# A hybrid encoder layer in split precision: both parts of the moving operand in one matmul

## The chip, the cores and the metric

The kernel runs on one core of a Trainium2 chip. The metric is the device time of one execution in microseconds (us), lower is better.

## The reference

One layer, 512 tokens, width 2048, float32. Three blocks with plain residual adds, each behind an RMSNorm, and a last RMSNorm:

```python
x = x + concat([gated_delta_net(h), short_conv(h)]) @ w_mix_out      # h = rmsnorm(x) @ w_mix_in
# cross-attention into 256 memory tokens, 4 heads of 512
q = h @ w_q;  k = mem_n @ w_k;  v = mem_n @ w_v
x = x + softmax(q @ k.T * 512 ** -0.5) @ v @ w_o
# ConvFFN, d_ff = 5632
u = causal_dwconv(h @ w_up, conv_w)                                  # width 3
x = x + (silu(u[..., :d_ff]) * u[..., d_ff:]) @ w_down
```

## The kernel before, in words

**Split precision.** A float32 operand is split in two: the high part is its rounding to the matmul's 4-byte format `fp32r` (a copy on ScalarE, ACT), the low part the rest (a subtraction on VectorE, DVE). A product is three matmuls into one PSUM bank: high x high, high x low, low x high. `wpiece` (line 133) loads 128 x 1024 weights through SP's DMA queue into one of 5 buffers `wst` and splits them into `whi` and `wlo`, 3 buffers each; `split` (147) does the same for a 128 x 512 tile of activations. `mm3` (153) issues the three matmuls, weights stationary and activations moving; `proj` (158) loops it over the depth.

**Stages.** Memory's K (`mem_proj`, 310; tile `psk`); the product of K and w_xq, "score weights", stored to `wk_d` (loop at 371, tile `pswk`); V (`mem_proj` again); V times w_xo to `mo_d`; the mixer's input projection with the delta net woven between; output projection; scores and softmax; the attention's output projection; the up-projection; the down-projection. In K, V, score weights and the up-projection the moving operand is 256 columns wide, in the other projections 512.

K and V: a bank holds two output blocks of 256 memory tokens each. They are multiplied by memory's norm `rmem` (DVE) and split. K's first three pairs wait for that norm in PSUM. Score weights: one bank of 512 columns per piece of w_xq, scaled by ACT on the way out.

**Up-projection.** A Strassen-like scheme with seven products per unit, on halves of the tokens (`LO`, `HI`, 256 columns each) and halves of the depth. The seven moving operands `xop[1..7]` are made by `up_prepare` (807) during the attention's output projection. The loop over 44 units (line 1050) alternates gate and up columns, a pair of units per tile of the hidden layer. `pair_loads` (844) fetches four weight blocks on SP's queue and forms two sums of weights by accumulating DMAs on GpSimd's (POOL's) queue (lines 853 and 859). A unit's products, each eight triples by `product` (910), run into banks in this order:

```python
px: 1 -> copied;  py: 2;  px += 6 -> copied;  pz: 5 -> copied
px += 7 -> added to pz's copy;  pz += 3;  px += 4
```

Partial sums leave by ACT copies (lines 1064, 1083, 1086: `tq`, `tz`) and DVE adds (1071, 1089, 1093: halves of `ug` and `uu`). `gate_half` (1019) multiplies by the FFN norm `r2`, convolves (`unit_conv`: one ACT and two DVE instructions) and applies Silu; `up_half` (1027) does norm and convolution for the up columns, multiplies by the gate, and on every second unit forms the sums that the down-projection needs; both store to `hf_d` on ACT's queue. Seven weight splits per unit (`wsplit`, 834: lines 837 and 838) run on ACT and DVE meanwhile.

**Order.** Each engine and each DMA queue works through its own list in order. A planner lays these lists out at build time: among the instructions whose inputs it reckons to be ready, by its own costs, it takes the one that stands first in the program. Inside `tc.manual_schedule(engines=...)` the named engines keep the program's order; that holds for PE in K, and for ACT and DVE in the last unit of the up-projection, where the first pieces of the down-projection (`make`, `fac_split`) are placed by hand between its steps.

PSUM has 8 banks: 3 in pool `pm`, 5 in `pg`. Tiles of 128 x 512 come from one pool of 64 (`T`), 56 of which hold `xop` in the up-projection.

Of the kernel before, what the change touches and what calls it, by code (L numbers as in the profile page):

```python
# [69 lines left out]
def trunk(ctx: ExitStack, tc: tile.TileContext, g):  # L70
# [82 lines left out]
    def mm3(ps, wh, wl, xh, xl, first, last):  # L153
        nc.tensor.matmul(ps, wh, xh, start=first, stop=False)  # L154
        nc.tensor.matmul(ps, wh, xl, start=False, stop=False)  # L155
        nc.tensor.matmul(ps, wl, xh, start=False, stop=last)  # L156

    def proj(src, xs, ps, kt=KT, per=8, ready=None):

        for i in range(kt // per):  # L160
            hi, lo = ready[i] if ready else wpiece(src(i))
            for k in range(per):
                kk = i * per + k
                xh, xl = xs[kk]
                mm3(ps, hi[:, k * P : (k + 1) * P], lo[:, k * P : (k + 1) * P], xh, xl, kk == 0, kk == kt - 1)

# [88 lines left out]
    def mem_parts(i):  # L255
        mh, ml = T("mwh", F32R), T("mwl", F32R)
        for k in range(2):
            sl = slice(k * NMEM, (k + 1) * NMEM)
            c = col(C_MEMN + 2 * i + k)
            nc.scalar.activation(mh[:, sl], m2s[i][:, sl], AF.Identity, scale=c)  # L260
            nc.vector.scalar_tensor_tensor(ml[:, sl], m2s[i][:, sl], c, f(mh)[:, sl], op0=ALU.mult, op1=ALU.subtract)
            mws.append((mh[:, sl], ml[:, sl]))

# [46 lines left out]
    def mem_proj(w, begin=False, beside=None):  # L310

        out, held = [], []
        for n2 in range(KT // 2):
            if begin and n2 == 0:
                ps = [PG("psk")[:, :NMEM] for _ in range(2)]
                for i in range(2):
                    for k in range(8):
                        for q in range(2):
                            hi, lo = early[q, 2 * i + k // 4]
                            c = slice(k % 4 * P, (k % 4 + 1) * P)  # L320
                            mm3(ps[q], hi[:, c], lo[:, c], *mws[8 * i + k], i == 0 and k == 0, i == 1 and k == 7)
# [12 lines left out]
            if begin and n2 < 2:  # L334
                continue
            if begin and n2 == 2:
                mem_norm()
            for ps in held:
                t = T("kt")
                for q in range(2):  # L340
                    nc.vector.tensor_tensor(t[:, q * NMEM : (q + 1) * NMEM], ps[q], rmem[:, q], op=ALU.mult)
                th, tl = T("kth", F32R), T("ktl", F32R)
                nc.scalar.copy(th, t)
                nc.vector.tensor_tensor(tl, t, f(th), op=ALU.subtract)
                for q in range(2):
                    out.append((th[:, q * NMEM : (q + 1) * NMEM], tl[:, q * NMEM : (q + 1) * NMEM]))
            held = []
            if beside:
                beside(n2)
        return out  # L350
# [3 lines left out]

    nc.vector.tensor_copy(mk[:, 0, 0:1], f(kts[0][0])[:, 0:1])
# [3 lines left out]
    nc.vector.tensor_copy(idb[:, 0, 0:1], f(kts[0][0])[:, 0:1])  # L359
    nc.sync.dma_start(idb, g["idb"])  # L360
# [8 lines left out]
    for i in range(3):  # L369
        load_x()  # L370
    for i in range(KT):
        load_x()
        add_squares(xacc, xts[i], i == 0)
        wkt = [T("wka"), T("wkb")]
        for q in range(2):
            hi, lo = wpiece(g["w_xq"][i, q])
            ps = PG("pswk")
            for hh in range(2):
                for k in range(4):
                    kk = (2 * q + hh) * 4 + k  # L380
                    kl = hh * 4 + k
                    mm3(ps[:, hh * NMEM : (hh + 1) * NMEM], hi[:, kl * P : (kl + 1) * P], lo[:, kl * P : (kl + 1) * P], kts[kk][0], kts[kk][1], k == 0, k == 3)
            nc.scalar.activation(wkt[q], ps, AF.Identity, scale=col(C_XN + i))
            nc.scalar.dma_start(wk_d[i][:, q * S : (q + 1) * S], wkt[q])
    r0 = rstd_rows([xacc])
# [14 lines left out]
    with tc.manual_schedule(engines={mybir.EngineType.PE}):  # L400
        for hd in range(XH):
            for ng in range(4):
# [4 lines left out]
                for q in range(2):  # L407
                    hi, lo = wpiece(g["w_xo"][hd, ng, q])
                    for mt in range(2):
                        for k in range(2):  # L410
                            kk = q * 2 + k
                            vh, vl = vts[hd * 4 + kk]
                            msl = slice(mt * P, (mt + 1) * P)
# [390 lines left out]

    b11 = []

    def up_prepare(k, xa, xb):
        tt = nc.vector.tensor_tensor
        tc_, td = TB("tc"), TB("td")
        tt(tc_[:, LO], xa[:, HI], xa[:, LO], op=ALU.subtract)  # L810
        tt(tc_[:, HI], xb[:, HI], tc_[:, LO], op=ALU.subtract)
        tt(td[:, LO], xa[:, HI], xb[:, HI], op=ALU.subtract)
        tt(td[:, HI], xb[:, LO], tc_[:, HI], op=ALU.subtract)
        if k % 2 == 0:
            b11[:] = [T("b11h", F32R), T("b11l", F32R)]
        sl = HI if k % 2 else LO
        bh, bl = b11
        nc.scalar.copy(bh[:, sl], xa[:, LO])
        tt(bl[:, sl], xa[:, LO], f(bh)[:, sl], op=ALU.subtract)
        xop[1].append((bh[:, sl], bl[:, sl]))  # L820
        for t, left, right in ((xb, 2, 3), (tc_, 5, 6), (td, 7, 4)):
            th, tl = split(t, "xo")
            xop[left].append((th[:, LO], tl[:, LO]))
            xop[right].append((th[:, HI], tl[:, HI]))

# [84 lines left out]
    def product(ps, w, r, first):  # L910

        hi, lo = w
        for k in range(HK):
            c = slice(k * P, (k + 1) * P)
            xh, xl = xop[r][k]
            nc.tensor.matmul(ps, hi[:, c], xh, start=first and k == 0, stop=False, skip_group_check=True)  # L916
            nc.tensor.matmul(ps, hi[:, c], xl, start=False, stop=False, skip_group_check=True)  # L917
            nc.tensor.matmul(ps, lo[:, c], xh, start=False, stop=k == HK - 1, skip_group_check=True)  # L918

# [91 lines left out]
    def unit_conv(u, t):  # L1011
# [5 lines left out]
        return cv  # L1017

    def gate_half(i, ug):
        tt(ug, ug, r2[0], op=ALU.mult)  # L1020
        cv = unit_conv(ug, i)
# [4 lines left out]

    def up_half(pos, px, uu, gate):
        i, k = up_order[pos], pos // 2
        tt(uu[:, LO], px, r2[0][:, LO], op=ALU.mult)
        tt(uu[:, HI], uu[:, HI], r2[0][:, HI], op=ALU.mult)  # L1030
        cv = unit_conv(uu, NF + i)
# [15 lines left out]
        nc.scalar.dma_start(hf_d[k, 5:7].rearrange("f p s -> p f s"), b.rearrange("p (f s) -> p f s", f=2))  # L1047

    for i in range(NF):
        if i == 1:  # L1050
# [5 lines left out]
        else:  # L1056
            a11, a12, a22, s1, s3, w1, w2 = first
        px = PG("px")[:, :S2]
# [4 lines left out]
        tq, tz = T("tq"), T("tz")  # L1063
        nc.scalar.copy(tq[:, LO], px)
        if i:
            w2 = wsplit(a12)
        py = PM("py")[:, :S2]
        product(py, w2, 2, True)
        turn_rest()
        ug, uu = T("ug"), T("uu")  # L1070
        tt(ug[:, LO], py, tq[:, LO], op=ALU.add)
        if i == 1:
# [9 lines left out]
        product(px, wsplit(s2), 6, False)  # L1082
        nc.scalar.copy(tq[:, HI], px)  # L1083
        pz = PG("pz")[:, :S2]
        product(pz, wsplit(s1), 5, True)
        nc.scalar.copy(tz[:, LO], pz)
        if i < NF - 1:
            product(px, wsplit(s3), 7, False)
            tt(uu[:, HI], px, tz[:, LO], op=ALU.add)
# [3 lines left out]
            tt(ug[:, HI], pz, tq[:, HI], op=ALU.add)  # L1093
            product(px, wsplit(a22), 4, False)
            if not r2:
                r2.append(rstd_rows([acc2]))
            up_half(i, px, uu, gate_half(up_order[i], ug))
            continue

        with tc.manual_schedule(engines={mybir.EngineType.Activation, mybir.EngineType.DVE}):  # L1100
# [4 lines left out]
            fac_split(0, 0)  # L1105
            tt(uu[:, HI], px, tz[:, LO], op=ALU.add)
            product(px, w4, 4, False)
            make(0)
            tt(ug[:, HI], pz, tq[:, HI], op=ALU.add)
            make(1)  # L1110
            gate = gate_half(up_order[i], ug)
            fac_split(0, 1)
            up_half(i, px, uu, gate)

# [188 lines left out]
```

## Time and profile before

| | us |
|---|---|
| median of 3 runs (2791.53 to 2795.15) | 2793.29 |
| the profiled execution | 2792.25 |
| its span, first to last instruction | 2790.4 |
| busy in the span: TensorE (PE) | 2755.7 |
| VectorE (DVE) | 1981.4 |
| ScalarE (ACT) | 1382.8 |
| GpSimd (POOL) | 266.9 |

In the rows of the timeline stand start and duration of an instruction, its engine, line, operation, and output <- inputs with their shapes; in square brackets the idle time of its engine before it, and what ended that. In rows of groups, the count, then busy time and mean ns of one, then idle time before them. In rows of waits: who waited, for whom, us in total, times, longest. Matmuls are pipelined, so that their durations overlap, and the time that one takes of PE is read from start to start. `PEld` is PE's loading of weights, which runs beside the matmuls.

### The profile page before, as it was taken

To read this page: it belongs to the slowest core of one execution; us is meant where nothing else is said; L and a number is where in the kernel's file an instruction comes from. 1 tells how busy PE (TensorE), PEld (TensorE's weight loads), DVE (VectorE), ACT (ScalarE), POOL (GpSimd) and SP (SyncE) were. 2 spreads that over 40 slices of the span, in tenths; PEclk is the share of its full clock that TensorE was granted. 3 is DMA by queue.
4 is the path that set the end of the run, shared out by engine and by line. 5 is a ranking of instruction groups with operands and counts; after the bars stand their busy time and mean duration, and the time that the engine had idled before them with its cause. 6 is when DMAs were issued, how large, how long until landed. Compare 5 with 4: busy or idle time off the path is not lost.

```text
span 2790.4 us, 43956 instructions
## 1 busy us (share of the span) xinstructions
PE 2755.7 (99%) x17277; PEld 2470.8 (89%) x17277; DVE 1981.4 (71%) x2979; ACT 1382.8 (50%) x1944; POOL 266.9 (10%) x258
## 2 busy tenths in 40 slices
PE   9999999999999999999999999999999999999997
PEld 9999878888788888888789999999999998888885
DVE  6546547878774334445678888888888888877877
ACT  6564644345443323234565555555555555454545
POOL 2120001012110000110120000000000000000211
PEclk9999999999999999999999999999999999999999
DMA  7785853333322234445556666676766675764976
GB/s 260 239 281 190 265 179 103 112 94 94 106 91 87 98 98 151 141 145 178 167 167 178 182 178 182 175 194 160 193 171 192 164 190 189 255 191 144 288 229 176
DMA packets 213952, 479.72 MB, mean 172 GB/s; under 512 B 26720, under 2 KB 94192, under 8 KB 213744
## 3 DMA queue, kind: packets, MB, share of 16 engines
q1 hardware_dynamic: 154688, 372.81, 40.6%
q0 software_dynamic: 20272, 62.94, 12.6%
q10 hardware_dynamic: 38784, 41.17, 4.2%
q8 instruction: 135, 2.21, 0.3%
q14 instruction: 73, 0.60, 0.1%
HBM read 424.13 MB, written 52.71 MB: 171 GB/s over the span
## 4 chain that ended last, share of the span: by engine, by line
PE 66%; DVE 2%; DMA 1%; issue 1%; ACT 1%; DVEq 0%; SPq 0%; ACTq 0%
PE px L916 6%; PE px L917 6%; PE px L918 6%; PE psd L1136 4%; PE psd L1134 4%; PE psd L1135 4%; PE pssc L154 3%; PE pssc L156 3%; PE pssc L155 3%; PE psx L155 3%; PE psx L154 3%; PE psx L156 3%; PE pz L918 3%; PE pz L917 3%; PE pz L916 3%; PE py L918 1%
## 5 line engine op out<-in xcount | busy, mean ns | idle before, releaser
L144 DVE TENSOR_TENSOR wlo<-wst,whi 128x1024 fp32r<-128x1024 f32 x316 | 389.2, 1233 | 329.5 <-ACT whi L143 328.6
L143 ACT CAST whi<-wst 128x1024 fp32r<-128x1024 f32 x316 | 331.7, 1051 | 554.6 <-PE pssc L155 140.0
L837 ACT CAST whi<-wst 128x1024 fp32r<-128x1024 f32 x177 | 185.6, 1049 | 271.4 <-PE px L917 143.5
L916 PE MATMUL px<-xoh,whi 128*128 128x256 f32 x1056 | 299.1, 283 | 1.2 <-ACT tq L1083 0.9
L918 PE MATMUL px<-xoh,wlo 128*128 128x256 f32 x1056 | 298.9, 283 | 0.0
L917 PE MATMUL px<-xol,whi 128*128 128x256 f32 x1056 | 298.8, 283 | 0.0
L838 DVE TENSOR_TENSOR wlo<-wst,whi 128x1024 fp32r<-128x1024 f32 x177 | 216.4, 1223 | 70.3 <-ACT whi L837 68.9
L1136 PE MATMUL psd<-wlo,hdh 128*128 128x512 f32 x616 | 241.0, 391 | 7.8 <-DVE wlo L958 7.8
L1135 PE MATMUL psd<-whi,hdl 128*128 128x512 f32 x616 | 239.9, 389 | 0.5 <-DVE hdl L150 0.5
L1134 PE MATMUL psd<-whi,hdh 128*128 128x512 f32 x616 | 239.9, 389 | 0.1
L916 PEld LDWEIGHTS px<-xoh,whi 128*128 128x128 f32 x1056 | 202.7, 192 | 1.8 <-ACT tq L1083 1.1
L917 PEld LDWEIGHTS px<-xol,whi 128*128 128x128 f32 x1056 | 202.7, 192 | 0.0
L918 PEld LDWEIGHTS px<-xoh,wlo 128*128 128x128 f32 x1056 | 202.7, 192 | 0.0
L918 PE MATMUL pz<-xoh,wlo 128*128 128x256 f32 x704 | 199.4, 283 | 0.9 <-DVE wlo L838 0.9
L916 PE MATMUL pz<-xoh,whi 128*128 128x256 f32 x704 | 199.4, 283 | 0.3 <-ACT whi L837 0.3
L917 PE MATMUL pz<-xol,whi 128*128 128x256 f32 x704 | 199.2, 283 | 0.0
L837 ACT CAST whi<-s 128x1024 fp32r<-128x1024 f32 x131 | 137.2, 1048 | 87.3 <-PE px L917 66.8
L955 ACT CAST whi<-wst 128x1024 fp32r<-128x1024 f32 x99 | 104.3, 1054 | 121.7 <-issue 62.5
L838 DVE TENSOR_TENSOR wlo<-s,whi 128x1024 fp32r<-128x1024 f32 x131 | 160.1, 1222 | 0.5 <-ACT whi L837 0.5
L154 PE MATMUL psq<-hh,whi 128*128 128x512 f32 x384 | 155.9, 406 | 0.0
L154 PE MATMUL pssc<-hh,whi 128*128 128x512 f32 x384 | 153.2, 399 | 0.0
L156 PE MATMUL psq<-hh,wlo 128*128 128x512 f32 x384 | 150.2, 391 | 0.0
(364 smaller groups left out, 7640.1 us busy)
## 6 DMA issues: line engine op xcount, KB each, us to landing
wst<-in_w_up SPq DMA_DIRECT2D x132, 512.0 KB, 4.8
wst<-in_w_dn SPq DMA_DIRECT2D x121, 512.0 KB, 4.4
wst<-in_w_mix SPq DMA_DIRECT2D x112, 512.0 KB, 3.4
s<-in_w_up POOLq DMA_DIRECT2D x87, 512.0 KB, 5.8
s<-in_w_up SPq DMA_DIRECT2D x43, 512.0 KB, 4.9
hid<-hf_d SPq DMA_DIRECT2D x77, 256.0 KB, 5.0
wst<-in_w_xq SPq DMA_DIRECT2D x32, 512.0 KB, 5.0
wst<-in_w_xv SPq DMA_DIRECT2D x32, 512.0 KB, 3.5
```

The lines of the kernel that those rows point to most:

```text
L143: nc.scalar.copy(hi, st)
L144: nc.vector.tensor_tensor(lo, st, f(hi), op=ALU.subtract)
L154: nc.tensor.matmul(ps, wh, xh, start=first, stop=False)
L156: nc.tensor.matmul(ps, wl, xh, start=False, stop=last)
L837: nc.scalar.copy(hi, t)
L838: nc.vector.tensor_tensor(lo, t, f(hi), op=ALU.subtract)
L916: nc.tensor.matmul(ps, hi[:, c], xh, start=first and k == 0, stop=False, skip_group_check=True)
L917: nc.tensor.matmul(ps, hi[:, c], xl, start=False, stop=False, skip_group_check=True)
L918: nc.tensor.matmul(ps, lo[:, c], xh, start=False, stop=k == HK - 1, skip_group_check=True)
L1134: nc.tensor.matmul(ps, xh, wh, start=first, stop=False)
L1135: nc.tensor.matmul(ps, xl, wh, start=False, stop=False)
L1136: nc.tensor.matmul(ps, xh, wl, start=False, stop=last)
```

## The change

A moving operand's high and low parts now lie side by side in one tile of 512 columns. `mm2` takes the place of `mm3` for K, V, score weights and the up-projection: the high weights against all 512 columns in one matmul, and the low weights against the high half, 256 columns, added into the bank's second half. The product is the sum of the bank's halves, which has to be formed on the way out.

- K and V: a bank per output block; the second half is copied out by ACT, added by DVE, then multiplied and split as before, per block.
- Score weights: a bank per 256 columns; ACT scales the second half, DVE scales the first and adds. The first four pieces of w_xq are taken in another order.
- Up-projection: copies and adds take whole banks (`ga`, `gb`, `ub`, `ua`), and the halves of each are added in SBUF by an accumulating DMA on POOL's queue (`together`); in the last unit by DVE, but for `ga`. `normed` multiplies by the norm. A unit's `up_half` now follows the second product of the next unit (`held_up`); `gate_half` stays at the unit's end.

```diff
+    def mm2(ps, wh, wl, x, first, last):
+        n = x.shape[1] // 2
+        nc.tensor.matmul(ps, wh, x, start=first, stop=False, skip_group_check=True)
+        nc.tensor.matmul(ps[:, n:], wl, x[:, :n], start=False, stop=last, skip_group_check=True)
...
-                bank = (PG if begin else PM)("psk")
-                ps = [bank[:, q * NMEM : (q + 1) * NMEM] for q in range(2)]
+                ps = []
                 for q in range(2):
+                    ps.append((PG if begin and n2 != 2 else PM)("psk"))
...
             for ps in held:
-                t = T("kt")
                 for q in range(2):
-                    nc.vector.tensor_tensor(t[:, q * NMEM : (q + 1) * NMEM], ps[q], rmem[:, q], op=ALU.mult)
-                th, tl = T("kth", F32R), T("ktl", F32R)
-                nc.scalar.copy(th, t)
-                nc.vector.tensor_tensor(tl, t, f(th), op=ALU.subtract)
+                    t, th = T("kt"), T("kth", F32R)
+                    lo = t[:, NMEM:]
+                    nc.scalar.copy(lo, ps[q][:, NMEM:])
+                    t = t[:, :NMEM]
+                    nc.vector.tensor_tensor(t, ps[q][:, :NMEM], lo, op=ALU.add)
+                    nc.vector.tensor_tensor(t, t, rmem[:, q], op=ALU.mult)
+                    nc.scalar.copy(th[:, :NMEM], t)
+                    nc.vector.tensor_tensor(th[:, NMEM:], t, f(th)[:, :NMEM], op=ALU.subtract)
...
+        for hh in range(2):
             ps = PG("pswk")
+            for k in range(4):
+                kl = hh * 4 + k
+                mm2(ps, hi[:, kl * P : (kl + 1) * P], lo[:, kl * P : (kl + 1) * P], kts[2 * q * 4 + kl], k == 0, k == 3)
+            wk = wkt[q][:, hh * NMEM : (hh + 1) * NMEM]
+            nc.scalar.activation(wk, ps[:, NMEM:], AF.Identity, scale=col(C_XN + i))
+            nc.vector.scalar_tensor_tensor(wk, ps[:, :NMEM], col(C_XN + i), wk, op0=ALU.mult, op1=ALU.add)
...
+    def beside(t):
+        o = T("xo", F32R)
+        nc.scalar.copy(o[:, LO], t)
+        nc.vector.tensor_tensor(o[:, HI], t, f(o)[:, LO], op=ALU.subtract)
+        return o
...
+        xop[1].append(beside(xa[:, LO]))
         for t, left, right in ((xb, 2, 3), (tc_, 5, 6), (td, 7, 4)):
-            th, tl = split(t, "xo")
+            xop[left].append(beside(t[:, LO]))
+            xop[right].append(beside(t[:, HI]))
...
+    def together(t):
+        nc.gpsimd.dma_start(t[:, LO], t[:, HI], accum_op=ALU.add)
+
+    def normed(a, b, s2):
+        u = T(s2)
+        for t, sl in ((a, LO), (b, HI)):
+            tt(u[:, sl], t[:, LO], r2[0][:, sl], op=ALU.mult)
+        return u
...
-        tt(ug[:, LO], py, tq[:, LO], op=ALU.add)
+        tt(ga, py, ga, op=ALU.add)
+        together(ga)
+        if held_up:
+            pos, ua, ub, gate = held_up.pop()
+            up_half(pos, normed(ua, ub, "uu"), gate)
...
-            tt(uu[:, HI], px, tz[:, LO], op=ALU.add)
+            tt(ub, px, ub, op=ALU.add)
+            together(ub)
...
-            tt(ug[:, HI], pz, tq[:, HI], op=ALU.add)
+            tt(gb, pz, gb, op=ALU.add)
+            together(gb)
             product(px, wsplit(a22), 4, False)
+            ua = T("ua")
+            nc.scalar.copy(ua, px)
+            together(ua)
...
-            up_half(i, px, uu, gate_half(up_order[i], ug))
+            gate = gate_half(up_order[i], normed(ga, gb, "ug"))
+            held_up.append((i, ua, ub, gate))
```

More of the change, by code (lines that the diff above doesn't have):

```diff
@@ L314, in mem_proj @@
             if begin and n2 == 0:
-                ps = [PG("psk")[:, :NMEM] for _ in range(2)]
+                ps = [PG("psk") for _ in range(2)]
                 for i in range(2):
@@ L320, in mem_proj @@
                             c = slice(k % 4 * P, (k % 4 + 1) * P)
-                            mm3(ps[q], hi[:, c], lo[:, c], *mws[8 * i + k], i == 0 and k == 0, i == 1 and k == 7)
+                            mm2(ps[q], hi[:, c], lo[:, c], mws[8 * i + k], i == 0 and k == 0, i == 1 and k == 7)
                 for i in range(1, KT // 2):
@@ L338, in mem_proj @@
             for ps in held:
-                t = T("kt")
                 for q in range(2):
-                    nc.vector.tensor_tensor(t[:, q * NMEM : (q + 1) * NMEM], ps[q], rmem[:, q], op=ALU.mult)
-                th, tl = T("kth", F32R), T("ktl", F32R)
-                nc.scalar.copy(th, t)
-                nc.vector.tensor_tensor(tl, t, f(th), op=ALU.subtract)
-                for q in range(2):
-                    out.append((th[:, q * NMEM : (q + 1) * NMEM], tl[:, q * NMEM : (q + 1) * NMEM]))
+                    t, th = T("kt"), T("kth", F32R)
[6 more added lines that the diff above has]
+                    nc.vector.tensor_tensor(th[:, NMEM:], t, f(th)[:, :NMEM], op=ALU.subtract)
+                    out.append(th)
             held = []
@@ L370, in trunk @@
         load_x()
[L371 to L376, printed above, removed]
-            ps = PG("pswk")
[L378 to L384, printed above, removed]
+    wkts = {}
+    for step in range(2 * KT):
+        i, q = ((0, 0), (1, 0), (0, 1), (1, 1))[step] if step < 4 else divmod(step, 2)
+        if i not in wkts:
+            load_x()
+            add_squares(xacc, xts[i], i == 0)
+            wkts[i] = [T("wka"), T("wkb")]
+        wkt = wkts[i]
+        hi, lo = wpiece(g["w_xq"][i, q])
+        for hh in range(2):
+            ps = PG("pswk")
+            for k in range(4):
[4 more added lines that the diff above has]
+            nc.vector.scalar_tensor_tensor(wk, ps[:, :NMEM], col(C_XN + i), wk, op0=ALU.mult, op1=ALU.add)
+        nc.scalar.dma_start(wk_d[i][:, q * S : (q + 1) * S], wkt[q])
     r0 = rstd_rows([xacc])
@@ L914, in product @@
             c = slice(k * P, (k + 1) * P)
[L915 to L918, printed above, removed]
+            mm2(ps, hi[:, c], lo[:, c], xop[r][k], first and k == 0, k == HK - 1)
     A11, NS2, A12 = 2, 3, 5
@@ L1057, in trunk @@
             a11, a12, a22, s1, s3, w1, w2 = first
-        px = PG("px")[:, :S2]
+        px = PG("px")
         product(px, w1, 1, True)
@@ L1082, in trunk @@
         product(px, wsplit(s2), 6, False)
-        nc.scalar.copy(tq[:, HI], px)
-        pz = PG("pz")[:, :S2]
+        gb = T("gb")
+        nc.scalar.copy(gb, px)
+        pz = PG("pz")
         product(pz, wsplit(s1), 5, True)
-        nc.scalar.copy(tz[:, LO], pz)
+        ub = T("ub")
+        nc.scalar.copy(ub, pz)
         if i < NF - 1:
             product(px, wsplit(s3), 7, False)
-            tt(uu[:, HI], px, tz[:, LO], op=ALU.add)
+            tt(ub, px, ub, op=ALU.add)
+            together(ub)
             if i:
@@ L1105, in trunk @@
             fac_split(0, 0)
-            tt(uu[:, HI], px, tz[:, LO], op=ALU.add)
+            tt(ub, px, ub, op=ALU.add)
+            tt(ub[:, LO], ub[:, LO], ub[:, HI], op=ALU.add)
             product(px, w4, 4, False)
             make(0)
-            tt(ug[:, HI], pz, tq[:, HI], op=ALU.add)
+            tt(gb, pz, gb, op=ALU.add)
+            tt(gb[:, LO], gb[:, LO], gb[:, HI], op=ALU.add)
             make(1)
-            gate = gate_half(up_order[i], ug)
+            gate = gate_half(up_order[i], normed(ga, gb, "ug"))
+            ua = T("ua")
+            nc.scalar.copy(ua, px)
             fac_split(0, 1)
-            up_half(i, px, uu, gate)
+            tt(ua[:, LO], ua[:, LO], ua[:, HI], op=ALU.add)
+            up_half(i, normed(ua, ub, "uu"), gate)
     def quad(s2):
```

45 lines of the change are left out of this document (18 added, 27 removed).

## The prediction

> **What bounds the kernel.** First the page's busy times and its slices, then what TensorE (PE) waited for, then stretches by stage.
>
> ```profile
> PE 2755.7 (99%) x17277; PEld 2470.8 (89%) x17277; DVE 1981.4 (71%) x2979; ACT 1382.8 (50%) x1944; POOL 266.9 (10%) x258
> PE   9999999999999999999999999999999999999997
> DVE  6546547878774334445678888888888888877877
> PEclk9999999999999999999999999999999999999999
> ```
> ```profile
> PE psd L1136 <- DVE wlo L958: 7.8, 7, 1.7
> PE pso L644 <- ACT vn L640: 2.7, 1, 2.7
> ```
> ```profile
> 110.00:190.00 80.00, 80.00 (x669) 80.00 (x668) 34.90 (x28) 52.53 (x69) 23.44 (x25) 1.00 0.93 311
> 190.00:254.00 64.00, 64.00 (x531) 63.52 (x530) 45.15 (x56) 30.95 (x35) 1.30 (x1) 1.00 0.58 195
> 1530.00:2300.00 770.00, 770.00 (x6419) 770.00 (x6419) 649.89 (x838) 424.70 (x535) 66.17 (x77) 1.00 0.67 181
> ```
>
> TensorE is busy for 99% of the span in every slice but the last, at the full granted clock. Its two largest waits total 10.5 us. In the stretches (columns PE, PEld, DVE, ACT, POOL, clock, DMA share, GB/s) of the score weights, the V projection and the up-projection, PE has no idle time. What shortens PE's own stream there shortens the span, until another engine becomes the limit; the nearest is VectorE (DVE) in the up-projection, 649.89 of 770 us, 84%.
>
> How long a matmul occupies PE is read from start to start, not from its duration. Timeline of PE, 256-wide (first and last of 172 steps) and 512-wide (178 steps):
>
> ```profile
> 1699.75 0.28 PE L916 MATMUL px<-xoh,whi 128*128 128x256 f32 x1
> ...
> 1720.39 0.28 PE L917 MATMUL px<-xol,whi 128*128 128x256 f32 x1
> ```
> ```profile
> 1209.64 0.39 PE L155 MATMUL psx<-ypl,whi 128*128 128x512 f32 x1
> ...
> 1249.99 0.39 PE L156 MATMUL psx<-yph,wlo 128*128 128x512 f32 x1
> ```
>
> That is 20.64/172 = 0.1200 us, and 40.35/178 = 0.2267 us. The 256 further columns cost 0.1067 us, so 256 columns alone explain 0.1067 of the 0.1200; 0.0133 us is paid per matmul, whatever its width.
>
> **The change, part by part.**
>
> *Matmuls.* Three 256-wide ones per k become one 512-wide (high weights against both parts) and one 256-wide: 0.2267 + 0.1200 = 0.3467 us for 0.3600, a saving of 0.0133 us per triple. Counts by group:
>
> ```profile
> L916 PE MATMUL px<-xoh,whi 128*128 128x256 f32 x1056 | 299.1, 283 | 1.2 <-ACT tq L1083 0.9 <-DVE uu L1089 0.4
> L916 PE MATMUL pz<-xoh,whi 128*128 128x256 f32 x704 | 199.4, 283 | 0.3 <-ACT whi L837 0.3
> L916 PE MATMUL px<-b11h,whi 128*128 128x256 f32 x352 | 100.0, 284 | 0.0
> L916 PE MATMUL py<-xoh,whi 128*128 128x256 f32 x352 | 99.6, 283 | 0.0
> L154 PE MATMUL psk<-mwh,whi 128*128 128x256 f32 x480 | 136.4, 284 | 0.0
> L154 PE MATMUL pswk<-kth,whi 128*128 128x256 f32 x256 | 72.4, 283 | 0.0
> L154 PE MATMUL psk<-mwh,ewh 128*128 128x256 f32 x32 | 9.2, 289 | 1.2 <-ACT ewh L149 1.2
> ```
>
> Up-projection: 1056 + 704 + 352 + 352 = 2464 triples, 32.9 us. K, V and score weights: 480 + 32 + 256 = 768 triples, 10.2 us. Together 43.1 us. A unit of the up-projection (seven products of eight triples) shrinks from 20.16 to 19.41 us. The ends: 43.1 if the constant part goes with each matmul dropped, and 0 if it grows with the width in a mixed stream, which no row shows. I take 43.1, since the two widths give it directly.
>
> The Trainium skill's page "TensorE: Matmul & The Clock Gate", section "Wait — 56ns, not 53.3ns?", puts the fixed part at about 2.5 ns per matmul; 3232 triples would then give 8.1 us instead of 43.1. The trace does not agree: 0.0133 us.
>
> *Start of K.* The first 32 triples run while PE still waits for their splits (1.2 us in the last row above), so their 0.4 us may be lost; I count it lost (+0.4; ends 0 and 0.4).
>
> *K and V evictions.* Per bank one more ACT copy of 256 columns and one more DVE add, at rows of 0.37 and 0.42 us (below); per pair of output blocks, PE's 11 us, DVE gains about 1 us on its 45.15 of 64. Hidden by PE; two banks per pair out of three or five leave one whole projection, 5.5 us, for emptying. If that cover went, the price would be 0.8 us per bank. Zero taken.
>
> *Score weights.* DVE gets two 256-wide multiply-adds per 2.77 us piece (0.84 us) on its 34.90 of 80: hidden. But the DMA engines are at 0.93 there. PE asks 3.4 us less time for the same bytes, a share of 0.97; between nothing and all of the 3.4 may be lost. I take 1.0, nearer the low end, since no wait for a load stands in the rows of this stretch. The new order of the first four pieces buys two pieces' time for the last K blocks; PE waits for none of them now, so zero.
>
> *Splits of the moving operand* (`beside`): the 512-wide copies and subtractions become 256-wide ones, twice as many. A half is not half the price (0.42 against 0.69 below), so DVE and ACT each pay about 0.2 us more per call; all but the last call lie beside the out-projection. +0.2.
>
> *Evictions of a unit.* DVE's rows in two neighbouring units:
>
> ```profile
> 1800.00:1820.16 20.16, 20.16 (x170) 20.16 (x170) 16.79 (x22) 11.09 (x14) 1.75 (x2) 1.00 0.61 161
> 1820.16:1840.32 20.16, 20.16 (x170) 20.16 (x170) 17.33 (x24) 11.19 (x14) 1.72 (x2) 1.00 0.71 194
> ```
> ```profile
> 1817.19 1.23 DVE L838 TENSOR_TENSOR wlo<-wst,whi 128x1024 fp32r<-128x1024 f32 x1
> 1819.11 0.42 DVE L1093 TENSOR_TENSOR ug<-pz,tq 128x256 f32<-128x256 f32 x1 [0.69 <-PE pz L918]
> 1819.57 0.69 DVE L1020 TENSOR_TENSOR ug<-ug,rsy 128x512 f32<-128x512 f32 x1
> ```
> ```profile
> L1083 ACT COPY tq<-px 128x256 f32<-128x256 f32 x44 | 16.2, 369 | 21.2 <-DVE s L1044 19.2 <-PE px L918 2.0
> ```
>
> Three PSUM adds go from 256 to 512 columns (3 x 0.27 = 0.81 us); four 256-wide products with the norm replace two 256-wide and one 512-wide (4 x 0.42 - 0.42 - 0.42 - 0.69 = 0.15). DVE goes from a mean of 17.06 to about 18.0 us in a unit of 19.4: 93%, 1.4 us free. ACT gets three copies from 0.37 to about 0.62 us and one new one, 1.4 us on 11.1: hidden. PSUM banks stay as many as before. DVE is close to the limit but still under it, so this costs nothing by itself; without that 1.4 us the price is DVE's 18.0 us per unit itself.
>
> *Four accumulating DMAs per unit on POOL's queue.* Rows: issues with their median time to landing over the up-projection, a small one from earlier, the queue, and POOL's own time for an issue:
>
> ```profile
> s<-in_w_up POOLq DMA_DIRECT2D x77, 512.0 KB, 5.8
> hf_d<-h ACTq DMA_DIRECT2D x19, 128.0 KB, 4.7
> ```
> ```profile
> gc_d<-gct POOLq DMA_DIRECT2D x1, 16.0 KB, 1.7
> ```
> ```profile
> q0 software_dynamic: 10953, 39.87, 29.9%
> ```
> ```profile
> 1815.80 0.87 POOL L853 DMA_DIRECT2D s<-in_w_up  x1 [6.94 <-DVE wlo L838]
> ```
>
> POOL issues two DMAs per unit now, six then: 5.2 of 19.4 us, hidden. On q0 a packet takes 0.299 x 770 x 16 / 10953 = 0.34 us, for 4 KB; the 512 new packets of 1 KB per unit, at an estimated 0.1 us each (a quarter of that and a little for the start), add 3.2 us per engine per unit: the DMA share goes from 0.67 to about 0.86. Weights are fetched into spare buffers ahead of their splits and PE has no idle time in the stretch, so this hides; a weight that comes late would cost PE up to its landing time, 5 to 6 us.
>
> The wait is the risk. `gate_half` multiplies the halves by the norm on DVE, and that instruction waits for the landing of `together(gb)`, which starts when the sum of pz is out, one product before the unit ends. Behind it in DVE's order stand the weight splits of the next unit, and PE waits for those. The landing should take between 1.7 and 5.8 us. DVE has other work in between, at least two weight splits (2.4 us) if the planner reckons with a similar landing. A wait d per unit that DVE cannot fill counts as DVE work: up to 19.4 - 18.0 = 1.4 us of d is free. I take 3.5 us to landing, between the 16 KB and the 128 KB row, so d of about 1: free, with 2 us over the whole stage for irregular places (ends 0 and the rival below).
>
> The Trainium skill's page "DMA: Bandwidth & Descriptors", section "Anatomy of one DMA — SWDGE (gpsimd) path", gives 2.0 us plus bytes over 436 GB/s for a DMA of this queue; the estimate for 128 KB is 2.3 us, by which d would be nil and the sum 2 us lower. The trace is slower where the two can be compared: 5.8 us against the page's 3.2 for 512 KB.
>
> *Tails moved back.* A unit's up half (normalising, convolution, product, its stores on ACT's queue) is done after the next unit's py is out, about 5.5 us later, with landings of ua and ub long past: no wait, no change of work. In POOL's FIFO ua's DMA stands among the next unit's weight sums and holds them up by 0.87 us each.
>
> *Last unit.* PE waits there for DVE already:
>
> ```profile
> 2353.75 0.50 PE L1136 MATMUL psd<-wlo,hdh 128*128 128x512 f32 x1 [1.72 <-DVE wlo L958]
> ...
> 2360.50 0.50 PE L1136 MATMUL psd<-wlo,hdh 128*128 128x512 f32 x1 [1.00 <-DVE wlo L958]
> ```
>
> DVE, written out by hand here, gets 0.81 + 0.15 us as above and two or three 256-wide adds of halves, 3 x 0.42: 2.2 us, all on the chain. I take 2.3, the end that charges all of it. Nothing is the low end; about twice as much is the high one, if unit 42's tail, which now falls into this unit, finds no gap in DVE.
>
> **Sum.** -43.1 + 0.4 + 1.0 + 0.2 + 2.0 + 2.3 = -37.2 us. The profiled execution took 2792.25 us, its span 2790.4; 2792.25 - 37.2 = 2755.1. The median of the runs, 2793.29, lies 1 us higher: 2756.
>
> **The rivals.**
>
> *DVE held at the landing: slower.* If the sum of gb lands as late as the 512 KB row, 5.8 us, and only 2 us of DVE work stand before its consumer, d is 3.8: a unit takes 18.0 + 3.8 = 21.8 us instead of 20.16, 43 units give +71, and K, V and score weights give -10.2: about 2792 + 71 - 10 + 6 = 2859. It decides from d = 1.4 + 37.2/43 = 2.3 us on. For it: DVE is in order, the share rises to 0.86, and POOL is held up to 7 us at one weight sum (6.94 above). Against it: the small transfers' rows, and that DVE has splits to do. Chance 0.25, most of it below 2830.
>
> *DVE at its limit, gain halved.* d near 1.9 makes a unit 19.9 us: 2755 + 0.5 x 43 = 2777. Chance 0.13.
>
> *The fixed part isn't saved.* If the constant 0.0133 us stays with the columns, PE's stream is as long as before and only the 5.9 us of costs remain: 2798; with the page's 2.5 ns, 2790. For it: no row shows mixed widths. Against it: both widths' pitches are steady over 170 and more steps. Chance 0.06, most of it within 0.2%.
>
> **How the numbers follow.** 0.2% is 5.6 us, about what can be told from no change. Likeliest, 0.56: 2756, own range 2748 to 2767. Faster: 0.56 + 0.12 of the halved gain = 0.68; same: 0.07, from the third rival and d near 2.3; slower 0.25. The range takes in the halved gain, no change and the milder half of the first rival: 2748 to 2830, with about 0.04 below and 0.13 above.
>
> **What would show it.** PE starts 0.2267 and 0.1200 us apart in turn; units 19.4 us apart; DVE near 93% in the up-projection with no large wait of DVE for a landed sum. Wrong if DVE's waits list the `ga` or `gb` DMA with tens of us, if PE waits for wlo in every unit, or if the pair of pitches sums to 0.36.

## The result, and the profile after

| | before | after |
|---|---|---|
| median (range), us | 2793.45 (2791.53 to 2795.15), 4 runs | 2962.58 (2959.62 to 2966.36), 4 runs |
| profiled execution: time, span | 2792.25, 2790.4 | 2965.06, 2963.1 |

The ratio after to before is 1.0607 [1.0590, 1.0624]: 6.1% slower. The forecast was 2756 us, in a range of 2748 to 2830.

First where the time lies, by the first matmul of a tile (us from the span's start):

| | before | after | stage, change |
|---|---|---|---|
| score weights begin (`pswk`) | 102.6 | 99.8 | |
| up-projection begins (`px`) | 1453.8 | 1447.1 | all before it: -6.7 |
| down-projection begins (`psd`) | 2345.9 | 2512.0 | up-projection 892.1 to 1064.9: +172.8 |
| end | 2790.4 | 2963.1 | down-projection 444.5 to 451.1: +6.6 |

A unit of the up-projection takes 24.20 us (1064.9 / 44) instead of 20.28; 19.41 was forecast. The page of after, the same rows as before (busy times, then tenths in 40 slices):

```profile
PE 2801.9 (95%) x14045; PEld 2347.8 (79%) x14045; DVE 2062.2 (70%) x3162; ACT 1435.8 (48%) x2092; POOL 416.8 (14%) x431
PE   9999999999999999999988889898888888999997
DVE  7686548788753344466777777777777777877877
PEclk9999999999999999999999999999999999999998
```

PE was full in every slice but the last; now it has gaps in most of slices 21 to 34, the up-projection. DVE there shows sevens where it had eights: it has more work per unit and still is idle for longer. No engine is at its limit, so the list of waits comes next (total us, times, longest; first DVE's and ACT's, then PE's):

```profile
ACT ucv L1027 <- DVE ug L1040: 201.2, 44, 7.1
DVE ug L1040 <- DMA gb<-gb: 196.9, 42, 7.1
```
```profile
PE px L162 <- ACT ga L1086: 117.7, 41, 5.2
PE psd L1174 <- DVE wlo L971: 8.4, 5, 3.6
PE psd L1172 <- ACT ua L1148: 1.3, 1, 1.3
```

The second row is what the forecast had named as its disproof: in 42 of the 44 units DVE stands for 4.7 us in the mean (196.9 / 42) at the product with the norm (`normed`, L1040), until the DMA that adds gb's halves has landed. ACT stands behind DVE for the same time (`unit_conv`, L1027), and PE behind ACT. One unit, the lists of DVE, POOL and ACT:

```profile
1803.05 0.68 DVE L1121 TENSOR_TENSOR gb<-pz,gb 128x512 f32<-128x512 f32 x1
1803.97 1.23 DVE L854 TENSOR_TENSOR wlo<-wst,whi 128x1024 fp32r<-128x1024 f32 x1 [0.24 <-ACT whi L853]
1805.23 1.22 DVE L1119 TENSOR_TENSOR wst<-wst,s 128x1024 f32<-128x1024 f32 x1
1806.38 0.42 DVE L1040 TENSOR_TENSOR ug<-ga,rsy 128x256 f32<-128x256 f32 x1
1812.07 0.43 DVE L1040 TENSOR_TENSOR ug<-gb,rsy 128x256 f32<-128x256 f32 x1 [5.28 <-DMA gb<-gb]
```
```profile
1801.82 0.86 POOL L869 DMA_DIRECT2D s<-in_w_up  x1 [6.99 <-DVE wlo L854]
1803.02 0.86 POOL L1034 DMA_DIRECT2D ub<-ub  x1 [0.33 <-issue]
1804.03 0.86 POOL L1034 DMA_DIRECT2D gb<-gb  x1 [0.15 <-issue]
1807.44 0.86 POOL L1034 DMA_DIRECT2D ua<-ua  x1 [2.56 <-ACT ua L1125]
```
```profile
1806.57 0.58 ACT L1125 COPY ua<-px 128x512 f32<-128x512 f32 x1
1812.53 0.72 ACT L1027 ACTIVATE ucv<-ug,cols 128x512 f32<-128x512 f32 x1 [5.38 <-DVE ug L1040]
1813.16 1.03 ACT L853 CAST whi<-s 128x1024 fp32r<-128x1024 f32 x1
1814.10 0.58 ACT L1086 COPY ga<-px 128x512 f32<-128x512 f32 x1
```

gb's sum is out at 1803.73. Behind it DVE does 2.9 us of other work (a split, a weight sum, ga's product), then waits 5.28 us: the DMA was issued at 1804.03 and the waiter starts at 1812.07, 8.0 us later. ACT's list has the convolution at its head, so the copy of the next unit's px into ga (L1086), which has nothing to do with gb, goes out at 1814.10. The sixth product reuses that px bank, so PE waits. PE's list at that place:

```profile
1810.96 0.28 PE L163 MATMUL py<-xo,wlo 128*128 128x256 f32 x1
1814.73 0.80 PE L162 MATMUL px<-xo,whi 128*128 128x512 f32 x1 [3.48 <-ACT ga L1086]
...
1815.53 0.63 PE L162 MATMUL px<-xo,whi 128*128 128x512 f32 x1
1815.96 0.41 PE L163 MATMUL px<-xo,wlo 128*128 128x256 f32 x1
1816.17 0.63 PE L162 MATMUL px<-xo,whi 128*128 128x512 f32 x1
```

After its idle 3.48 us PE runs a pair in 0.64 us (1815.53 to 1816.17) instead of 0.347. The stretches say why (PE, PEld, DVE, ACT, POOL, granted clock, DMA share, GB/s):

```profile
1811.00:1814.70 3.70, 0.24 (x2) 0.00 (x0) 2.59 (x4) 2.17 (x4) 0.00 (x0) 0.95 0.31 49
1814.70:1817.70 3.00, 2.97 (x9) 2.59 (x10) 3.00 (x6) 3.00 (x4) 0.86 (x1) 0.50 0.25 19
1817.70:1820.00 2.30, 2.30 (x14) 2.00 (x14) 2.30 (x4) 0.94 (x1) 0.86 (x1) 1.00 0.84 146
```

The granted clock is 0.50 in the middle row. By the trace's clock records that stretch begins at 1814.31, while PE still waits, and lasts 3.41 us. The whole up-projection adds up so:

```profile
1445.00:2505.00 1060.00, 934.95 (x4906) 800.50 (x4906) 787.03 (x1011) 524.66 (x668) 226.53 (x260) 0.93 0.72 169
```

4906 matmuls are 2453 pairs, 850.5 us at 0.3467. PE is busy for 934.95, so 84.5 us went into matmuls that ran slower, most of it at the reduced clock (0.50 for 153.6 us in 33 stretches, in which PE was busy for 138), and 125.05 us it was idle. DVE's 787.03 of 1060 us is 17.97 us per unit; 18.0 had been forecast. With the wait of 4.7 its unit is at 22.7 us; the rest to 24.2 is waits for ACT's casts and for PE.

How long the four DMAs took from issue to landing, over 1500 to 2300 us:

```profile
q0 software_dynamic: 28512, 51.92, 39.8%
...
s<-in_w_up POOLq DMA_DIRECT2D x66, 512.0 KB, 6.8
...
ga<-ga POOLq DMA_DIRECT2D x33, 128.0 KB, 4.3
ub<-ub POOLq DMA_DIRECT2D x33, 128.0 KB, 9.0
gb<-gb POOLq DMA_DIRECT2D x33, 128.0 KB, 7.4
ua<-ua POOLq DMA_DIRECT2D x33, 128.0 KB, 4.8
```

The 128 KB that are added inside SBUF take 4.3 to 9.0 us, the weight sums with four times the bytes 6.8. The slow two, ub and gb, follow a weight sum on the same queue, in the unit shown within 2.2 us (`s` at 1801.82 in POOL's rows above). Each of the 33 gb sums of this stretch was issued while that weight sum was under way, and landed after it, by 2.0 us in the median. But the weight sum ahead is not the whole of it: in the run with the gate held back (below), ub and gb go out with no weight sum under way and still take 7.6 and 5.9 us in the median, ga 2.7. What else delays them was not tried.

### The profile page after: what moved, and what is told of

It is laid out like the page before. It is cut to its first block, busy times and chain, and to the rows that moved or that the text cites. A ratio compares the mean times of both kernels' runs of the same rounds, so it can differ in the third digit from the quotient of the medians.

```text
span 2963.1 us, 38426 instructions
## 1 busy us (share of the span) xinstructions
PE 2801.9 (95%) x14045; PEld 2347.8 (79%) x14045; DVE 2062.2 (70%) x3162; ACT 1435.8 (48%) x2092; POOL 416.8 (14%) x431
## 4 chain that ended last, share of the span: by engine, by line
PE 34%; DMA 17%; DVE 11%; issue 7%; POOL 2%; ACT 1%; POOLq 0%; DVEq 0%; SPq 0%; ACTq 0%
DMA gb<-gb 10%; DMA s<-in_w_up 5%; DVE wlo L854 5%; PE psd L1174 4%; PE psd L1173 4%; PE psd L1172 4%; PE pssc L154 3%; DVE ucv L1029 3%; PE pssc L156 3%; PE pssc L155 3%; PE psx L154 3%; PE psx L155 3%; PE psx L156 3%; POOL ub L1034 1%; DVE uu L1040 1%
## 5 line engine op out<-in xcount | busy, mean ns | idle before, releaser
L162 PE MATMUL px<-xo,whi 128*128 128x512 f32 x1408 | 560.9, 433 | 120.8 <-ACT ga L1086 117.7
L162 PEld LDWEIGHTS px<-xo,whi 128*128 128x128 f32 x1408 | 292.2, 208 | 204.6 <-ACT ga L1086 130.8
L163 PE MATMUL px<-xo,wlo 128*128 128x256 f32 x1408 | 421.3, 299 | 2.3 <-DVE wlo L854 2.3
L163 PEld LDWEIGHTS px<-xo,wlo 128*128 128x128 f32 x1408 | 294.9, 209 | 5.2 <-DVE wlo L854 5.1
L162 PE MATMUL pz<-xo,whi 128*128 128x512 f32 x704 | 253.2, 399 | 1.0 <-ACT whi L853 1.0
L163 PE MATMUL pz<-xo,wlo 128*128 128x256 f32 x704 | 197.8, 281 | 0.9 <-DVE wlo L854 0.9
L162 PE MATMUL psk<-mw,whi 128*128 128x512 f32 x480 | 167.6, 394 | 0.0
L162 PEld LDWEIGHTS pz<-xo,whi 128*128 128x128 f32 x704 | 134.3, 191 | 33.5 <-ACT whi L853 1.3
L1040 DVE TENSOR_TENSOR ug<-gb,rsy 128x256 f32<-128x256 f32 x44 | 18.7, 425 | 196.9 <-DMA gb<-gb 196.9
```

Source lines behind the costliest of these rows:

```text
L162: nc.tensor.matmul(ps, wh, x, start=first, stop=False, skip_group_check=True)
L163: nc.tensor.matmul(ps[:, n:], wl, x[:, :n], start=False, stop=last, skip_group_check=True)
```

## The experiments

From the comparison of the two traces, theory A: DVE is held at landed sums because the planner places the consumer of a landing where it reckons that the data is there, and reckons too early; the 512-wide matmul saves what was forecast. Rivals, B: a consumer that stands later in the program is later on DVE, so one removed wait ends it; C: the lowered clock is the cost, and an even PE would be faster; D: the mixed widths save little by themselves. (These letters hold for the text; an expectation's rivals A and B are its own.)

**The halves of gb added by DVE, the other three DMAs kept.**

```diff
-            together(gb)
+            tt(gb[:, LO], gb[:, LO], gb[:, HI], op=ALU.add)
```

> One DMA of the four per unit is replaced: gb's halves are added by DVE (one 256-wide add, 0.34 us between starts), the three other DMAs stay. Theory (landing of gb holds DVE, DVE holds ACT, ACT holds the copy of px, PE stands and its clock is lowered): the wait of DVE for gb, 197 us, is gone, a unit falls from 24.2 to 19.4 or a little more, the kernel to 2755 to 2775. Rival A (DVE is simply over its limit by the wider adds): DVE has still more to do, 2962 or more. Rival B (the load of four DMAs on the queue delays weights): a quarter of the loss goes, about 2920.

Measured: 2837.27 us, 1.0161 [1.0148, 1.0175] to before. The wait for gb is gone, and 125 us with it, but the kernel is still slower than before. DVE's largest wait over 1500 to 2250 us, and PE's:

```profile
DVE uu L1040 <- DMA ua<-ua: 90.6, 36, 3.5
```
```profile
PE px L163 <- DVE wlo L854: 33.9, 34, 1.1
```

DVE waits 2.5 us a unit for ua, whose tail had been "moved back" behind the next unit's py. The wait changed its name. The expectation, which took gb for the only late landing, was wrong by 62 us at its near end.

**The gate's half held back a unit as well, in the program alone.**

```diff
-            pos, ua, ub, gate = held_up.pop()
+            pos, ha, hb, ua, ub = held_up.pop()
+            gate = gate_half(up_order[pos], normed(ha, hb, "ug"))
...
-            gate = gate_half(up_order[i], normed(ga, gb, "ug"))
-            held_up.append((i, ua, ub, gate))
+            held_up.append((i, ga, gb, ua, ub))
```

> The gate half is moved back beside the up half: normed(ga, gb), its convolution and Silu follow the next unit's second product too. All four DMAs and all DVE work stay. Theory (landing of gb): the landing has about 8 us more before its consumer, so 2755 to 2775. Rival A (DVE over its limit): no change, 2962. Rival B (load of the DMAs): no change, 2962.

Measured: 2942.57 us, 1.0536 [1.0522, 1.0551]: 20 us less than the kernel after, and far from the 2755 to 2775 of the expectation. DVE's list in one unit:

```profile
1806.65 0.42 DVE L1040 TENSOR_TENSOR ug<-ga,rsy 128x256 f32<-128x256 f32 x1
1809.27 0.42 DVE L1040 TENSOR_TENSOR ug<-gb,rsy 128x256 f32<-128x256 f32 x1 [2.19 <-DMA gb<-gb]
1813.22 0.42 DVE L1040 TENSOR_TENSOR uu<-ua,rsy 128x256 f32<-128x256 f32 x1 [3.53 <-DMA ua<-ua]
...
1815.03 0.68 DVE L1092 TENSOR_TENSOR ga<-py,ga 128x512 f32<-128x512 f32 x1
```

In the program all these products follow the sum of py (L1092); on DVE they stand ahead of it, and DVE waits at two of them. This decides between A and B: the place in the program is a preference among what the planner reckons to be ready, and it reckoned these ready.

**The 512-wide form in K, V and score weights alone**, the up-projection as before (`beside` and the products of the up-projection in their old form, the rest of the change left).

> The new matmul form in K, V and score weights alone; the up-projection as in the kernel before. Theory: that part of the forecast holds, 768 triples by 0.0133 us less about 2 us, so 2784 to 2787 (ratio 0.9965 to 0.998). Rival (that part loses too, by its evictions or its loads): 2793 or more.

Measured: 2786.94 us, 0.9982 [0.9973, 0.9991], 4.5 us less than before (2791.42). The up-projection starts at 1447.4 us, 6.4 earlier; by the steps of the forecast it was 8.6.

**The kernel after, with PE kept busy:** twelve 512-wide matmuls into a spare bank behind the second product of each unit, at 0.2267 us each 2.7 us of PE per unit.

```diff
+            idle = PM("idle")
+            for _ in range(12):
+                nc.tensor.matmul(v4(idle), onesr, onesr.unsqueeze(1).broadcast_to([P, 4, P]), start=True, stop=True)
```

> The changed kernel with 12 more matmuls of 512 columns (2.7 us at full clock) on every unit from the second, after its second product, in a spare bank: useless work in the place where PE stands 2.7 us per unit. Theory that the clock lowered after the wait costs time by itself (0.50 granted for some 3 us after it): the wait is filled, the clock stays, some 1.6 us per unit come back, about 2890. Rival (the lowered clock is hidden in the chain of the landing): 2962. Rival (PE's own time is the bound there): 2962 + 43 x 2.7 = 3078.

Measured: 3008.64 us, 1.0765 [1.0745, 1.0784], between the numbers of the two rivals. Over 1500 to 2250 us the granted clock is 0.97 instead of 0.93, and the unit is 25.2 us: DVE still waits for gb, and PE's wait moved to another of ACT's copies:

```profile
DVE ug L1040 <- DMA gb<-gb: 125.7, 29, 5.8
```
```profile
PE px L162 <- ACT gb L1112: 53.3, 30, 2.2
```

C is not borne out: with most of the clock back, no time came back. But the fill is itself work ahead of the sixth product, so what the lowered clock costs by itself stays open. That a late landing costs without it, the run with gb on DVE shows: its granted clock is 1.00 over 1500 to 2250 us, and its unit takes 21.3 us all the same.

**Without the late landings, three ways.** All four adds by DVE (the body of `together` becomes `tt(t[:, LO], t[:, LO], t[:, HI], op=ALU.add)`):

> All four pairs of halves are added by DVE, 256 columns each; no accumulating DMA of sums is left. Theory (DVE waits for landings because the planner puts the consumer where it reckons the landing, earlier than it is): no such wait is left and DVE has 18.0 + 4 x 0.34 = 19.4 us of work in a unit of 19.4 on PE, so DVE and PE run neck and neck, unit 19.5 to 20.3, 2760 to 2800. Rival (what holds DVE are the wider adds and the norm's four products, whatever the DMAs do): at least the 21.1 us per unit of the run with gb on DVE, 2837 or more.

gb and ua by DVE, ga and ub by DMA:

> gb and ua are added by DVE, ga and ub by DMA as before. Theory: the wait for ua (2.5 us per unit in the run with gb alone on DVE) goes as the wait for gb went; ub has landed by then, so DVE does 18.7 us per unit with little waiting: unit 19.4 to 20.0, 2755 to 2785. Rival (a wait moves on to the next DMA, ub, at the same length): about 2837.

All four by DMA, the gate's and the up half's operations held back and tied on DVE behind the sum of py of the next unit by an issue-order edge, not by the program's order alone:

```diff
-        tt(ga, py, ga, op=ALU.add)
+        after_this = tt(ga, py, ga, op=ALU.add)
...
+            before = held_up.pop()
+            with tc.issue_after(after_this.ins):
+                finish(*before)          # gate_half and up_half of the unit before
```

> As the run with the gate held back, but with an edge that keeps the norm's products and what DVE does after them behind the sum of py in DVE's order. All four DMAs stay. Theory (the planner had moved these instructions up to where it reckoned the landing): gb has 5.5 us more, ua about 5 us from its issue against a landing of 5 to 6, so a short wait for ua stays: unit 19.5 to 21, 2765 to 2830. Rival (program place alone decides, the planner kept it): no change from that run, 2942.

And the same, tied behind the sum of ub, some 8 us later, with one tile more for ug (in the last unit, which has no such tie, they follow the sum of py in the program alone):

> All four DMAs stay; normalising, convolution and the rest of both halves are kept in DVE's order behind the sum of px and pz (ub) of the next unit, 8 us later than in the run with the edge at py; one more tile of 2 KB per partition for ug. Theory: every landing has 10 us or more, DVE waits for none of them and has 18.0 us in 19.4: 2755 to 2770, the forecast. Rival A (DVE over its limit): 2837 or more. Rival B (DMA load): 2800 or more, with waits for weights.

| halves added by | held behind | us | ratio to before | unit, us | DVE share, PE busy of 750 us |
|---|---|---|---|---|---|
| DVE all four | - | 2770.50 | 0.9919 [0.9891, 0.9946] | 19.62 | 98%, 750.00 |
| DVE gb, ua; DMA ga, ub | - | 2773.77 | 0.9928 [0.9912, 0.9945] | 19.96 | 93%, 748.58 |
| DMA all four | sum of py | 2789.73 | 0.9991 [0.9981, 1.0000] | 20.28 | 88%, 740.67 |
| DMA all four | sum of ub | 2771.65 | 0.9929 [0.9914, 0.9944] | 19.89 | 89%, 746.45 |

(A unit is the stage over 44; the last two columns are from 1500 to 2250 us of one execution each.) The stretch of the first and of the last kernel of the table:

```profile
1500.00:2250.00 750.00, 750.00 (x4329) 655.88 (x4328) 737.03 (x1046) 463.56 (x580) 66.14 (x77) 1.00 0.71 186
```
```profile
1500.00:2250.00 750.00, 746.45 (x4241) 644.53 (x4240) 667.09 (x873) 465.25 (x569) 197.40 (x228) 1.00 0.88 209
```

The first three lie in the range of their first theory, the last 1.65 us above it. D falls with the first row, for this execution: 4329 matmuls in 750 us, PE without a gap, with DVE at 98%; the last section has executions that save half as much. A holds: once DVE no longer stands at a landing, whether the DMAs are gone or their consumers are tied later, the 170 us and more are gone. With the tie behind py, DVE's waits for landings were 0.3 us in all, but ACT's copy of gb then came late (PE 9.3 us in that stretch); tied 8 us later, DVE waits for no landing at all and the DMAs are as good as DVE's own adds. In the mixed version DVE still waits 41.4 us for ub in 36 units, and PE hardly notices, 1.3 us in all: here the wait lies beside other work.

**The last unit in the old form,** to see what the end of the stage costs: in unit 43 three 256-wide matmuls, 256-wide copies and sums, no adds of halves. Once on the all-DVE kernel, once on the one tied behind ub, with the all-DVE kernel again beside them.

> All halves added by DVE, as in the kernel with the one line of together changed, but the last up unit (23, whose end is ordered by hand) in the old form: three 256-wide matmuls, 256-wide copies and sums, no adds of halves. Theory A: the last unit's loss is the work that the change adds to DVE and ACT at the transition into the down-projection (three adds of halves, four copies and three sums twice as wide, some 3.5 us of DVE by its rows). Then the time from the last unit's first matmul to the hundredth psd matmul falls by 2 to 5 us and PE's waits for DVE wlo and ACT ua at the first psd shrink to before's; the unit's 96 triples cost 1.3 us more; net 1 to 4 us less than the all-DVE kernel, 2767 to 2770. Theory B: the transition is bound by the splits of the first factors and weights, which neither changes: the time stays or is 1 us worse, 2770 to 2772.

> The kernel with four DMAs and the held operations a whole step later (2771.65 us), with the last up unit in the old form, as the other kernel of this call. Theory A: 1 to 4 us less, 2768 to 2771. Theory B: 2771 to 2773.

> The all-DVE kernel once more on the same chip as the other two: 2770.5 us before, both theories 2768 to 2772.

Measured: 2763.90 us, 0.9894 [0.9872, 0.9916]; 2775.13, 0.9938 [0.9927, 0.9950]; all-DVE again 2769.10, 0.9914 [0.9893, 0.9934]. The first lies below theory A's range, the second above both ranges, the third in its own. Between the first and the third the intervals overlap, so the medians don't tell them apart. But the times of the all-DVE kernels fall into two groups (last section), and in each the old last unit is faster: medians 2756.1 against 2761.2 us, and 2772.5 against 2776.1 (three times each against five). The traces agree, for that place: from the last unit's first matmul to the hundredth psd matmul 46.3 us pass instead of 50.4 (46.0 before the change), a fall inside theory A's 2 to 5; the down-projection takes 446.0 instead of 451.8 us (444.5 before the change), and PE's waits at its first matmuls, in the 62 us from 6 us before its start, are (last unit old; then all-DVE):

```profile
PE psd L1179 <- DVE wlo L977: 3.1, 2, 2.1
```
```profile
PE psd L1174 <- DVE wlo L971: 3.6, 1, 3.6
PE psd L1172 <- ACT ua L1148: 1.2, 1, 1.2
```

With the longer wait comes a lower clock. The 6.75 us that begin 10.4 us behind the down-projection's first matmul are, with the last unit old, then all-DVE:

```profile
2335.25:2342.00 6.75, 5.73 (x26) 4.39 (x25) 6.75 (x14) 2.62 (x4) 0.00 (x0) 1.00 1.03 321
```
```profile
2321.75:2328.50 6.75, 5.65 (x13) 4.47 (x14) 6.75 (x13) 1.62 (x3) 0.00 (x0) 0.50 0.86 273
```

At a clock of 0.50 PE starts 13 matmuls instead of 26, which is 2.9 us behind at 0.2267 us each. The first of the three has the lowest median of all versions, 1.1% below before. In the second, with the DMAs, the gain is lost again ahead of it. Unit 42's operations, held back, fall into the last unit, and DVE waits there for ua:

```profile
2303.24 0.42 DVE L1046 TENSOR_TENSOR uu<-ua,rsy 128x256 f32<-128x256 f32 x1 [2.33 <-DMA ua<-ua]
```
```profile
2307.17 0.58 PE L935 MATMUL px<-xo,wlo 128*128 128x256 f32 x1 [4.17 <-DVE wlo L854]
```

So the cost of the last unit is the work that its new form adds to DVE and ACT, as theory A of that run had it, together with the lower clock behind PE's wait, on the kernel without DMAs; neither theory foresaw the second.

## Why the prediction was wrong

**The step that failed: the landing of gb's sum.** The forecast named the place, the instruction and the rival, and gave that rival 0.25. It sized the landing at 3.5 us, between the rows of a 16 KB (1.7) and a 128 KB DMA (4.7), with the 512 KB row (5.8) as the far end. Measured: 7.4 us in the median, beyond the far end. The 128 KB row was a plain store on another queue. gb's DMA instead stands behind a 512 KB accumulation and another sum on its own queue; how much of the 7.4 us is due to that stays open, since gb took 5.9 us with no weight sum under way. DVE's other work was estimated rightly (2.4 us; 2.9 in the unit shown), so the wait d is 4.7 us where "about 1" was taken and 1.4 was free. The rows at hand allowed better: POOL's weight sums, the only accumulating DMAs of that stage, took 5.8 us, and were the nearest kind; with 5.8 for the landing and 2.4 of other work d is 3.4, still short of the 4.7.

**The rival was too cheap as well.** With d = 4.7 its own formula gives 18.0 + 4.7 = 22.7 us per unit, and 2792 + 43 x (22.7 - 20.16) - 10 + 6 = 2897 us. The unit took 24.2. What it lacked is the other path: it had PE wait for weight splits behind DVE (3.2 us in the up-projection), while PE waited for ACT's copy of px (117.7 us), which stands behind a convolution that stands behind DVE; and PE's clock then was 0.50 for 3.41 or 6.83 us behind most of these waits.

**"Tails moved back: no wait".** Wrong. With gb out of the way ua became the wait (2.5 us a unit), ahead of the place the program gives it. The text assumed that a later place in the program is a later place on DVE.

**What held.** The matmul term: 0.0133 us per triple is what the all-DVE kernel shows, in the stretch from 2285.85 to 2294.52 us 25 pairs, 0.3468 us each:

```profile
2285.85 0.40 PE L162 MATMUL px<-xo,whi 128*128 128x512 f32 x1
...
2294.52 0.39 PE L162 MATMUL py<-xo,whi 128*128 128x512 f32 x1
```

It didn't hold in every execution (last section). DVE's 18.0 us per unit was 17.97; the DMA share of "about 0.86" was 0.88 where units run at 19.9 us; and PE's stream through score weights and V stays without gaps:

```profile
110.00:270.00 160.00, 160.00 (x920) 140.04 (x919) 122.43 (x176) 103.69 (x162) 23.46 (x25) 1.00 0.79 257
```

**Sizes that were off.** K, V and score weights: -8.6 forecast, -6.7 measured at the start of the up-projection (-6.4 in the kernel with that part alone). The last unit: +2.3 forecast, with 4.6 as the high end; the down-projection is 6.6 us longer, and the old form of the last unit gave 5.8 of 7.3 back where no DMA is involved. Of that, 1.2 us is PE's wait for ACT's copy of ua, 0.5 a longer wait for `wlo`, and some 2.9 the lower clock behind it (rows above); how the rest splits was not measured.

With landings out of the way the forecast of 2756 was missed by 13 to 16 us still (2769 to 2772). Of that K, V and score weights and the last unit explain about 6; for the all-DVE kernel, about half of whose executions took some 15 us longer than the others, the last section has the rest.

## What to carry to other kernels

A small DMA inside SBUF was not a cheap add here: its price is its landing, 4.3 to 9.0 us by place. The nearest row for it was a DMA of the same queue and the same kind (accumulating, 5.8 us), not one of the same size, and even that was too short. DVE, which takes its list in order, paid for it. Where a planner places instructions by its own idea of a landing, moving an operation later in the program need not move it on the engine. Tie it with an order, or give the add to the engine itself: 0.42 us of DVE four times a unit made the kernel 190 us faster than four DMAs that take no time of DVE's, but whose results DVE waited for. And when an engine is held, follow every list behind it (DVE, then ACT, then PE) before pricing the wait.

## What the hardware showed that was not expected

**The clock after a gap.** PE idle for 3.48 us is followed by a granted clock of 0.50, in a stage that ran at 1.00 before. In the unit shown the clock falls before PE starts again, and in the up-projection it stays at 0.50 for 3.41 us (21 times) or 6.83 us (12 times). The 512-wide matmuls are then 0.43 us apart, the 256-wide 0.21 (the rows of PE's list above). The Trainium skill's page "TensorE: Matmul & The Clock Gate", section "Part 1: The HAM clock gate", has two states, full and half clock: half after at least one idle window of about 3.4 us, full after a busy one. The trace agrees with the two states and with the window's length, 3.41 us. It does not agree that PE has to be idle for that long: the half clock followed waits of PE as short as 2.1 us, though not every one; they are 2.9 us in the mean and 5.2 at most.

**A pair of 512 and 256 columns has more than one pitch.** The same instructions without a gap, in the profiled execution of the kernel with the last unit in the old form:

```profile
1849.57 0.40 PE L162 MATMUL px<-xo,whi 128*128 128x512 f32 x1
...
1855.93 0.40 PE L162 MATMUL px<-xo,whi 128*128 128x512 f32 x1
```

18 pairs in 6.36 us: 0.3533 us each, half of the saving, at a granted clock of 1.00, through the whole stage. Over its 2408 pairs (the last unit has none) that is 16 us more than at 0.3467. The times of the all-DVE kernels fall into two groups that fit: 2755.6 to 2764.9 us in eight executions, 2770.4 to 2776.6 in eight; those of before, with its 256-wide triples, lie between 2787.7 and 2795.2. In the kernels that use the DMAs the mean pair in a sample of 160 us (gaps left out) was 0.349 to 0.353 us. What picks the pitch of an execution was not found; it leaves the question why the best kernels miss 2756 answered in size only.
